# First conditioning product in two column halves, key projections between them, and conditioning steps of one load

## The chip, the cores and the metric

The kernel runs as one program on one core of a Trainium2 chip. The metric is the device time of an execution in microseconds (us). A timing is the median of several runs, and a profile is one further execution recorded by the hardware profiler.

The engines are TensorE (PE in the profile; PEld is its weight loading), VectorE (DVE), ScalarE (ACT), GpSimd (POOL) and SyncE (SP). SyncE issues every DMA of this kernel from one queue, in order.

## The reference

The reference is one inference step of a two-layer encoder trunk with width 1024. It handles a prompt of 1024 positions and eight sample sequences of 16 positions, 1152 token rows in all. Every sub-layer is modulated by a conditioning vector `c`: one vector for the prompt and one for each sample sequence, nine rows in all. This is the part that the change touches:

```python
sc = jax.nn.silu(c)
ada = (sc @ w_ada[l] + b_ada[l])[:, None, :]
sh_m, sc_m, g_m, sh_f, sc_f, g_f = jnp.split(ada, 6, axis=-1)
h = x * (1 + sc_m) + sh_m
qkv = h @ w_qkv_a[l]
...
x = layer_norm(DEEPNORM_ALPHA * x + (1 + g_m) * mix, ln_g[l, 0], ln_b[l, 0])
h = x * (1 + sc_f) + sh_f
f, conv_rows = conv_ffn(h, None if prompt else state_conv[l], w_up[l], conv_w[l], conv_b[l], w_down[l])
x = layer_norm(DEEPNORM_ALPHA * x + (1 + g_f) * f, ln_g[l, 1], ln_b[l, 1])
```

Layer 0 attends within a window, with 16 query heads and four key/value heads (256 key columns, 256 value columns), learned sinks, and a table of relative biases. Between the layers one key/value pair of width 1024 is projected, with a shift and a scale of its own. Layer 1 attends in a band. Each layer ends in a gated MLP of width 2816 with a causal convolution. In all there are seven conditioning products of 1024 x 2048: three per layer and one for the key/value pair.

## The kernel before

**Layout.** `H` holds the modulated input, transposed, as high and low halves: `split` (L166) copies a value to a rounded type (L157 or L159) and subtracts that copy from the value (L168). A product is then three matmuls for each slice of the contraction: weight-low by input-high, weight-high by input-low, weight-high by input-high. `mmT` (L267, matmul L272) takes 24 of them for a block of 384 tokens and 128 output columns; `mmX` (matmul L284) does the same with tokens on the output partitions. Weights come through `wload` (L170): a 512 KB load into one of two staging slots (`ws`), and a split into `wh` and `wl` on ScalarE and, by default, GpSimd.

**Order.** The program is written in one order, and a planner with a modelled timeline reorders the instructions of each engine's queue, the DMA queue included. On the chip every queue runs in the order it was given. `issue_after` ties an instruction behind another one, `high_priority` raises it, and `keep_in_program_order` fixes it among others so marked.

**A conditioning product, `ada` (L197).** The conditioning vectors, padded to 32 columns, are the stationary operand. For each of eight slices of the contraction, two loads of 512 KB bring 128 x 2048 weights, and four matmuls of 512 columns (L216) write four strips of 32 partitions of one PSUM bank, one strip of the array each. One step of the generator is one slice with its two loads. Then the bias comes, broadcast by four DMAs (L205), VectorE adds it (L228), TensorE transposes the row (L241), and VectorE copies nine columns for each 128 features into `adaT` (L243). Products 1, 2, 5 and 6 also send a gate row to DRAM.

**Opening, `build` (L1192).** Product 0 (shift and scale of layer 0) takes 16 weight loads, with the first key weight after six slices and the first of three blocks of x behind the last one; then follow its bias, the second key weight and the two other blocks. When `adaT` is complete, `affine` (L246) forms scale and shift (L253, L255). `first_h` (L1176) scales x: 24 tiles, eight 128-feature slices `c` in each of three blocks, on ScalarE (L1187), with the 128 sample rows of the third block on GpSimd (`sample_affine`, L917 and L918), and the splits into `H` on VectorE. Then come the key projections (`kproj`, six times 24 matmuls), the value projections (`vproj`, 216 matmuls of 256 columns), the first query projections (72 matmuls), and the scores (L514, L517). Keys and values go through DRAM (`kH`, `vH`) and back, and the biases through a skewed table in DRAM (`ska`) that `tables` (L1146) prepares. For the sample sequences, L648 makes their scores with four matmuls in four column strips, 144 columns wide in layer 0 and 272 in layer 1.

**Background.** Products 1 and 2 run as generators beside the attention of layer 0, one step each time an accumulated rate `BGA` passes one, with the two `ws` slots as their ring. Products 3 to 6 run beside the MLP of layer 0 at rate `BGF` per weight load, with a ring of three other buffers.

Of the kernel before, what the change touches and what calls it, by code (L numbers as in the profile page):

```python
# [10 lines left out]
F32 = mybir.dt.float32  # L11
# [22 lines left out]
BGA = 0.33  # L34
BGF = 0.72
# [59 lines left out]
class Trunk:  # L95
# [101 lines left out]
    def ada(self, gi, bank, ring=None, row=None):  # L197
# [3 lines left out]

        def load_bias(row):
            bsrc = self.I["adab"][gi : gi + 1, :]
            for j in range(4):
                nc.sync.dma_start(  # L205
                    row[32 * j : 32 * j + 32, 512:1024],
                    bass.AP(bsrc.tensor, bsrc.offset + j * 512, [[0, 32], [1, 512]]),
                )

        early = row is not None  # L210
        for k in range(8):
            w = [ring.next() for _ in range(2)]
            for hf in range(2):
                nc.sync.dma_start(w[hf], self.I["adaw"][gi, k, hf])
            for j in range(4):
                nc.tensor.matmul(  # L216
                    ps[32 * j : 32 * j + 32, :],
                    self.cT[:, k * 32 : k * 32 + 32],
                    w[j // 2][:, (j % 2) * 512 : (j % 2) * 512 + 512],
                    start=k == 0,  # L220
                    stop=k == 7,
                    tile_position=(0, 32 * j),
                )
            yield
        if not early:
            row = ring.next()
        load_bias(row)
        nc.vector.tensor_add(row[:, 0:512], ps, row[:, 512:1024])  # L228
        yield
        gate = {1: (0, 0), 2: (1, 2), 5: (2, 0), 6: (3, 2)}.get(gi)  # L230
        if gate is not None:
            g, j0 = gate
            for j2 in range(2):
                r = slice(32 * (j0 + j2), 32 * (j0 + j2) + 32)
                nc.gpsimd.tensor_scalar_add(row[r, 512:1024], row[r, 0:512], 1.0)
                nc.sync.dma_start(
                    self.gd[g, :, j2 * 512 : j2 * 512 + 512],
                    row[32 * (j0 + j2) : 32 * (j0 + j2) + 9, 512:1024],
                )
        for i in range(4):  # L240
            nc.tensor.transpose(ps[:, i * 128 : i * 128 + 128], row[:, i * 128 : i * 128 + 128], self.ident)  # L241
        dst = self.adaT[:, gi * 144 : gi * 144 + 144].rearrange("p (j i r) -> p i j r", j=4, i=4)
# [50 lines left out]
    def kproj(self, l, c, w, banks, tmp):  # L293
# [3 lines left out]
        for bi, (s0, n) in enumerate(BLK):  # L297
# [17 lines left out]
            if n > m:  # L315
                nc.sync.dma_start(self.kS[l][rows, :], t[:, m:n])
# [875 lines left out]
    def build(self):  # L1192
# [13 lines left out]
        for _ in range(6):  # L1206
            next(a0)
# [152 lines left out]
```

## Time and profile before

| | us |
|---|---|
| median of 3 runs | 2977.12 |
| lowest and highest run | 2976.96, 2980.3 |
| profiled execution | 2971.91 |
| its span | 2970.1 |
| PE, PEld busy in the span | 2849.4, 2529.7 |
| DVE, ACT, POOL busy | 1537.9, 1135.8, 911.0 |

The table sums one core's engines over the whole span. Busy matmul time overlaps itself in the pipeline, so PE at 96% of the span is not PE at its peak. The mean TensorE clock granted was 0.984 of full speed. DMA moved 353.90 MB. The opening, in which the DMA engines are loaded most, is the first 2.5% of the span.

In a row of the timeline the columns are start, length, engine, line, operation, output and input, shape, count, and in brackets the idle time before it and what ended it. A matmul of this kernel's plain 32-bit kind (L216, L648) leaves two records in the trace, so a step of four matmuls counts x8. In a row of groups the columns are line, engine, operation, names, shapes and count, then busy us and mean ns of one, then the idle time before them and what ended it.

### The profile page before, as it was taken

Reading aid. Unit: us, or ns where it says so; the run is one execution under the profiler, and the core shown is the slowest. Engines: PE = TensorE matmul, PEld = TensorE weight load, DVE = VectorE, ACT = ScalarE, POOL = GpSimd, SP = SyncE. Lnnn points to the kernel's source line nnn. Section 1 sums busy time; section 2 is a strip of 40 time slices with the busy share of each in tenths; the row PEclk is TensorE's granted clock in tenths of the full one; section 3 lists DMA queues with packets and bytes.
Section 4 is the critical chain, followed back from the end, with each engine's and each line's share of the span. In section 5 each row is a group of like instructions: output and inputs, shape, how many; then the busy total and the mean of one; then the engine's idle time right before and its main releaser. Section 6 shows DMA issues by size and latency. Waiting matters only on the chain.

```text
span 2970.1 us, 42557 instructions
## 1 busy us (share of the span) xinstructions
PE 2849.4 (96%) x16326; PEld 2529.7 (85%) x16326; DVE 1537.9 (52%) x3336; ACT 1135.8 (38%) x2352; POOL 911.0 (31%) x661
## 2 busy tenths in 40 slices
PE   6999899999999999999999999889999999999997
PEld 4987668899888898997999888767999999999986
DVE  4376768333443343459312667667724444444468
ACT  2465634332222222224435666652442222222224
POOL 3132423222222221254651111231422222222253
PEclk8999889999999999999999999999999999999998
DMA  8546353622222212223885456663311111111121
GB/s 302 182 146 188 100 167 127 227 76 77 97 71 99 92 69 75 82 71 110 285 289 181 121 151 192 185 209 126 133 43 43 43 40 42 43 43 38 41 83 77
DMA packets 175963, 353.90 MB, mean 119 GB/s; under 512 B 34680, under 2 KB 91832, under 8 KB 175504
## 3 DMA queue, kind: packets, MB, share of 16 engines
q1 hardware_dynamic: 175760, 351.19, 36.0%
q8 instruction: 128, 2.10, 0.3%
q14 instruction: 75, 0.61, 0.1%
HBM read 285.22 MB, written 75.35 MB: 121 GB/s over the span
## 4 chain that ended last, share of the span: by engine, by line
PE 80%; DVE 8%; DMA 3%; ACT 2%; issue 2%; POOL 2%; SPq 0%; DVEq 0%; ACTq 0%; POOLq 0%
PE PS L272 46%; PE PS L1065 16%; PE PS L284 7%; PE PS L564 3%; PE PS L542 2%; PE PS L216 2%; PE PS L514 1%; PE PS L517 1%; DVE F L481 1%; PE PS L683 1%; DMA F<-in_adaw_dram 1%; DVE acc L1125 1%; DVE F L954 0%; POOL acc L1124 0%; POOL wl L168 0%
## 5 line engine op out<-in xcount | busy, mean ns | idle before, releaser
L272 PE MATMUL PS<-H,wh 128*128 128x384 f32 (+1 forms) x5472 | 1045.4, 338 | 0.1
L272 PEld LDWEIGHTS PS<-H,wh 128*128 128x128 f32 x5472 | 966.7, 188 | 18.1 <-issue 7.9
L168 POOL TENSOR_TENSOR wl<-ws,wh 128x1024 fp32r<-128x1024 f32 x167 | 405.3, 2432 | 744.6 <-ACT wh L157 680.5
L994 DVE SCALAR_TENSOR_TENSOR F<-PS,F 128x256 f32<-128x256 f32 (+2 forms) x704 | 353.0, 512 | 533.2 <-ACT F L991 520.1
L272 PE MATMUL PS<-H,wl 128*128 128x384 f32 (+1 forms) x2736 | 565.0, 343 | 17.6 <-DVE H L159 8.2
L272 PEld LDWEIGHTS PS<-H,wl 128*128 128x128 f32 x2736 | 489.0, 190 | 49.9 <-issue 15.1
L991 ACT ACTIVATE F<-PS,F 128x384 f32<-128x384 f32 x264 | 177.5, 672 | 746.8 <-PE PS L272 745.2
L1065 PE MATMUL PS<-wh,X 128*128 128x512 f32 x1320 | 412.4, 394 | 9.6 <-DVE acc L1056 4.1
L1056 DVE TENSOR_TENSOR acc<-acc,PS 128x512 f32<-128x512 f32 x324 | 221.7, 686 | 271.6 <-PE PS L1065 271.1
L1040 POOL TENSOR_TENSOR F<-F 128x384 f32<-128x384 f32 x132 | 138.1, 1046 | 647.3 <-ACT F L1038 645.4
L1065 PEld LDWEIGHTS PS<-wh,X 128*128 128x128 f32 x1320 | 245.8, 188 | 63.1 <-issue 6.7
L157 ACT CAST wh<-ws 128x1024 fp32r<-128x1024 f32 x174 | 180.0, 1045 | 148.5 <-PE PS L1065 75.9
L1065 PE MATMUL PS<-wl,X 128*128 128x512 f32 x660 | 217.0, 393 | 0.0
L284 PE MATMUL PS<-wh,H 128*128 128x256 f32 (+1 forms) x936 | 170.4, 311 | 3.3 <-DVE H L168 2.3
L1065 PEld LDWEIGHTS PS<-wl,X 128*128 128x128 f32 x660 | 124.3, 188 | 28.1
L284 PEld LDWEIGHTS PS<-wh,H 128*128 128x128 f32 x936 | 135.0, 192 | 13.3 <-DVE H L168 3.0
L168 DVE TENSOR_TENSOR X<-F,X 128x384 fp32r<-128x384 f32 x110 | 97.1, 883 | 89.6 <-ACT X L157 89.3
L602 POOL TENSOR_TENSOR F<-F,x2att 64x512 f32<-64x512 f32 x62 | 79.3, 1279 | 191.4 <-DVE F L578 162.5
L542 PE MATMUL PS<-C,F 128*128 128x128 f32 x720 | 115.2, 286 | 20.7 <-DVE wh L549 11.4
L284 PE MATMUL PS<-x1att,H 128*128 128x512 f32 x504 | 132.4, 406 | 1.1 <-ACT x1att L157 0.5
L1038 ACT ACTIVATE F<-F 128x384 f32<-128x384 f32 x132 | 69.2, 524 | 143.7 <-DVE F L994 129.5
L542 PEld LDWEIGHTS PS<-C,F 128*128 128x128 f32 x720 | 85.4, 145 | 42.8 <-DVE wh L549 14.7
(213 smaller groups left out, 3448.0 us busy)
## 6 DMA issues: line engine op xcount, KB each, us to landing
ws<-in_wup_dram SPq DMA_DIRECT2D x88, 512.0 KB
F<-in_adaw_dram SPq DMA_DIRECT2D x74, 512.0 KB
ws<-in_wdn_dram SPq DMA_DIRECT2D x44, 512.0 KB
ws<-in_adaw_dram SPq DMA_DIRECT2D x32, 512.0 KB
x1att<-kH SPq DMA_DIRECT2D x60, 256.0 KB
xd<-F SPq DMA_DIRECT2D x27, 512.0 KB
F<-xd SPq DMA_DIRECT2D x27, 512.0 KB
vH<-X SPq DMA_DIRECT2D x40, 256.0 KB
```

The lines of the kernel that those rows point to most:

```text
L157: nc.scalar.copy(out, in_)
L168: self.eng(el).tensor_sub(lo, src, hi.bitcast(F32))
L272: self.nc.tensor.matmul(out[:, 0:n], w[a][:, k * 128 : k * 128 + 128], H[:, p, k, s0 : s0 + n], start=i == 0, stop=i == 23)
L284: self.nc.tensor.matmul(out[:, 0:n], H[:, p, j * kn + k, t0 : t0 + 128], w[a][:, k * n : k * n + n], start=i == 0, stop=i == 23,)
L542: nc.tensor.transpose(t[:, n * 128 : n * 128 + 128], p[:, (kt - k0) * 128 : (kt - k0) * 128 + 128], self.ident)
L564: mm = nc.tensor.matmul(ob[:, i0 * 128 : (i0 + n) * 128], vst[a][:, kt, :], pp[:, m * 128 : (m + n) * 128], start=cnt == 0, stop=cnt == to ...
L602: self.eng("v" if last else "p").tensor_mul(on[r, q], on[r, q], rb[r, :])
L991: nc.scalar.activation(y, ps[:, off : off + 384], AF.Identity, bias=w(3), scale=w(2))
L994: nc.vector.scalar_tensor_tensor(o, u, w(i), o, op0=ALU.mult, op1=ALU.add)
L1040: nc.gpsimd.tensor_mul(a, y, ya[bi])
L1056: nc.vector.tensor_add(row[:, n], row[:, n], ps)
L1065: nc.tensor.matmul(ps, ac[m][p][:, cs], w[m][q][:, n], start=i == 0, stop=i == 5)
```

## The change

- **Product 0** is made in two halves of its columns by a new function, `ada_half`. Half `h` holds shift and scale of the feature slices 4h to 4h + 3, and the weight columns are laid out on the host so that each half is eight loads of 512 KB. A half ends with its own add, two transposes, and the copies that form scale and shift, at high priority.
- **`opening`** replaces the start of `build`. It writes the loads in a fixed order: the weights of half 0, with the bias rows (two DMAs in place of four, from an array already broadcast on the host), the sinks and the first key weight among them; half a block of x; the second key weight; another half block; then the weights of half 1 with further half blocks of x between. x goes in 12 DMAs of 384 KB. All three blocks have buffers of their own.
- **Key projections** are split along the contraction: `mmT_part` with part 0 takes slices 0 to 3 as soon as half 0 is done, part 1 takes the rest, and six PSUM banks hold the partial sums. `kstore` is the second half of the old `kproj`. The second key weight's low part is made on VectorE in place of GpSimd.
- **`ada`** for products 1 to 6: one step is one load of 512 KB, with four matmuls of 256 columns that are tied behind the first of them and raised. The tail copies in two pieces. A gate row takes one GpSimd add in place of two, and four stores in place of two.
- **Rates**: `BGA` from 0.33 to 0.6 and `BGF` from 0.72 to 1.3, for about twice as many steps.
- The silu of the conditioning is computed for the nine used columns only, the rest being set to zero.

The diff, cut to its core:

```diff
-BGA = 0.33
-BGF = 0.72
+BGA = 0.6
+BGF = 1.3
...
-    def ada(self, gi, bank, ring=None, row=None):
+    def ada(self, gi, bank, ring=None):
+        lead = [None] * 4
         for k in range(8):
+                w = ring.next()
+                nc.sync.dma_start(w, self.I["adaw"][gi, k, hf])
+                for j in range(4):
+                    with ExitStack() as es:
+                        if lead[j] is not None:
+                            es.enter_context(self.tc.issue_after(lead[j]))
+                        if j:
+                            es.enter_context(self.tc.high_priority())
+                            es.enter_context(self.tc.issue_after(first))
+                        mm = nc.tensor.matmul(
+                            ps[32 * j : 32 * j + 32, hf * 256 : hf * 256 + 256],
+                            self.cT[:, k * 32 : k * 32 + 32],
+                            w[:, j * 256 : j * 256 + 256],
+                            start=k == 0 and hf == 0,
+                            stop=k == 7 and hf == 1,
+                            tile_position=(0, 32 * j),
+                            skip_group_check=True,
+                        )
+                    first = mm.ins if j == 0 else first
+                    lead[j] = lead[j] or mm.ins
+                yield
+        row = ring.next()
+        bsrc = self.I["adab"][gi : gi + 1, :]
+        for j in range(4):
+            nc.sync.dma_start(
+                row[32 * j : 32 * j + 32, 512:1024].rearrange("p (h x) -> p h x", h=2),
+                bass.AP(bsrc.tensor, bsrc.offset + j * 256, [[0, 32], [1024, 2], [1, 256]]),
+            )
         nc.vector.tensor_add(row[:, 0:512], ps, row[:, 512:1024])
         yield
+        gate = {1: (0, 0), 2: (1, 1), 5: (2, 0), 6: (3, 1)}.get(gi)
+            g, hf = gate
+            nc.gpsimd.tensor_scalar_add(row[:, 512:768], row[:, hf * 256 : hf * 256 + 256], 1.0)
+            for j in range(4):
+                nc.sync.dma_start(self.gd[g, :, j * 256 : j * 256 + 256], row[32 * j : 32 * j + 9, 512:768])
             nc.tensor.transpose(ps[:, i * 128 : i * 128 + 128], row[:, i * 128 : i * 128 + 128], self.ident)
+        dst = self.adaT[:, gi * 144 : gi * 144 + 144].rearrange("p (h j i r) -> p h i j r", h=2, j=4, i=2)
+        src = ps.rearrange("p (h i j r) -> p h i j r", h=2, i=2, j=4)
+        for h in range(2):
+            nc.vector.tensor_copy(dst[:, h], src[:, h, :, :, 0:9])
         yield
...
+    def mmT_part(self, w, out, s0, n, part):
+        for k in range(4 * part, 4 * part + 4):
+            for a, p in ((1, 0), (0, 1), (0, 0)):
+                self.nc.tensor.matmul(
+                    out[:, 0:n],
+                    w[a][:, k * 128 : k * 128 + 128],
+                    self.H[:, p, k, s0 : s0 + n],
+                    start=k == 0 and a == 1,
+                    stop=k == 7 and a == 0 and p == 0,
+                )
...
-            for c in range(2):
-                self.kproj(l, c, wk[c], kvb, kvt)
+            for bi, (s0, n) in enumerate(BLK):
+                for c in range(2):
+                    ps = self.bank(2 * bi + c)
+                    self.mmT_part(wk[c], ps, s0, n, 1)
+                    self.kstore(0, c, bi, ps, kvt)
...
-        ps = self.bank(1)
+        ps = self.bank(6)
...
-        s = I["sinks"]
-        nc.sync.dma_start(self.sink[:, 0:16], bass.AP(s.tensor, s.offset, [[0, 128], [1, 16]]))
-        nc.sync.dma_start(self.sink[:, 16:18], I["sinkS"])
-        nc.vector.tensor_scalar_mul(self.sink, self.sink, -1.0)
-        nc.sync.dma_start(self.sinkH, I["sinkH"])
...
+    def load(self, dst, src):
+        self.tc.keep_in_program_order(self.nc.sync.dma_start(dst, src))
+    def ada_half(self, h, bank, ring, row, t):
+        ps = self.bank(bank)
+        for k in range(8):
+            w = ring.next()
+            self.load(w, self.I["adaw"][0, k, h])
+            for j in range(4):
+                nc.tensor.matmul(
+                    ps[32 * j : 32 * j + 32, 0:256],
+                    self.cT[:, k * 32 : k * 32 + 32],
+                    w[:, j * 256 : j * 256 + 256],
+                    start=k == 0,
+                    stop=k == 7,
+                    tile_position=(0, 32 * j),
+            yield
+        with self.tc.high_priority():
+            nc.vector.tensor_add(row[:, 0:256], ps[:, 0:256], row[:, 256:512])
+            for i in range(2):
+                nc.tensor.transpose(ps[:, i * 128 : i * 128 + 128], row[:, i * 128 : i * 128 + 128], self.ident)
+            dst = self.adaT[:, 0:144].rearrange("p (w h c i r) -> p h i w c r", w=2, h=2, c=2, i=2)
+            src = ps[:, 0:256].rearrange("p (i w c r) -> p i w c r", i=2, w=2, c=2)
+            for i in range(2):
+                nc.vector.tensor_copy(dst[:, h, i], src[:, i, :, :, 0:9])
+            c = slice(36 * h, 36 * h + 36)
+            nc.vector.tensor_scalar_add(t[:, c], self.adaT[:, 72 + 36 * h : 72 + 36 * h + 36], 1.0)
+            nc.vector.tensor_copy(t[:, 72 + 36 * h : 72 + 36 * h + 36], self.adaT[:, c])
+    def first_h(self, t, x3, bi, h):
+        nc = self.nc
+        G, B = (t[:, o : o + 72].rearrange("p (c r) -> p c r", r=9) for o in (0, 72))
+        s0, n = BLK[bi]
+        m = min(n, 1024 - s0)
+        c0 = 4 * h
+        if n > m:
+            xm = x3[:, c0 : c0 + 4, m:n]
+            self.sample_affine(xm, xm, G, B, c0, 4, "p")
+        for c in range(c0, c0 + 4):
+            nc.scalar.activation(x3[:, c, 0:m], x3[:, c, 0:m], AF.Identity, bias=B[:, c, 0:1], scale=G[:, c, 0:1])
+            self.split(x3[:, c, :], self.H[:, 0, c, s0 : s0 + n], self.H[:, 1, c, s0 : s0 + n], "v", "v")
+    def opening(self):
+        nc, I = self.nc, self.I
+        ct = self.F[:, 12288:12544]
+        nc.sync.dma_start(ct, I["cT"])
+        row = [self.F[:, 10240 + 512 * h : 10752 + 512 * h] for h in range(2)]
+        ring = Ring([self.F[:, i * 1024 : i * 1024 + 1024] for i in range(10)])
+        x1 = self.x1p.tile([128, 9216], F32, name="x1in", tag="x1")
+        xs = [x1[:, i * 3072 : i * 3072 + 3072].rearrange("p (c t) -> p c t", t=384) for i in range(3)]
+        nc.gpsimd.memset(self.cT, 0.0)
+        s3, c3 = (t.rearrange("p (k r) -> p k r", r=32)[:, :, 0:9] for t in (ct, self.cT))
+        nc.scalar.activation(c3, s3, AF.Exp, scale=-1.0)
+        nc.vector.tensor_scalar_add(c3, c3, 1.0)
+        nc.vector.reciprocal(c3, c3)
+        nc.vector.tensor_mul(c3, c3, s3)
+        def xload(bi, h):
+            for c in range(4 * h, 4 * h + 4, 2):
+                self.load(xs[bi][:, c : c + 2, :], I["xT"][bi, :, c : c + 2, :])
+        def run(g, n):
+            for _ in range(n):
+                next(g, None)
+        t = self.gbr.next()
+        a = [self.ada_half(h, 6 + h, ring, row[h], t) for h in range(2)]
+        run(a[0], 4)
+        for h in range(2):
+            self.load(row[h][:, 256:512], I["adab0"][h])
+        s = I["sinks"]
+        self.load(self.sink[:, 0:16], bass.AP(s.tensor, s.offset, [[0, 128], [1, 16]]))
+        self.load(self.sink[:, 16:18], I["sinkS"])
+        self.load(self.sinkH, I["sinkH"])
+        nc.vector.tensor_scalar_mul(self.sink, self.sink, -1.0)
+        run(a[0], 2)
+        wk = [self.wload(I["wk0"][0], el="v")]
+        run(a[0], 2)
+        xload(0, 0)
+        wk.append(self.wload(I["wk0"][1], el="v"))
+        run(a[0], 1)
+        xload(1, 0)
+        for bi in range(3):
+            if bi < 2:
+                run(a[1], 4)
+            if bi == 0:
+                xload(2, 0)
+            if bi == 1:
+                xload(0, 1)
+            self.first_h(t, xs[bi], bi, 0)
+            s0, n = BLK[bi]
+            for c in range(2):
+                self.mmT_part(wk[c], self.bank(2 * bi + c), s0, n, 0)
+        run(a[1], 1)
+        xload(1, 1)
+        xload(2, 1)
+        nc.sync.dma_start(self.lnT, I["lnT"])
+        for bi in range(3):
+            self.first_h(t, xs[bi], bi, 1)
+        return wk
...
+        wk = self.opening()
...
+    aw = [w.reshape(8, 128, 2, 1024).transpose(0, 2, 1, 3) for w in aw]
+    aw[0] = aw[0].reshape(8, 2, 128, 2, 512).transpose(0, 3, 2, 1, 4).reshape(8, 2, 128, 1024)
+    z["adaw"] = np.stack(aw)
+    ab = g["b_ada"][0][:2048].reshape(2, 2, 2, 1, 256).transpose(1, 0, 2, 3, 4)
+    z["adab0"] = c(np.broadcast_to(ab, (2, 2, 2, 32, 256)).reshape(2, 128, 256))
```

More of the change, by code (lines that the diff above doesn't have):

```diff
@@ L200, in ada @@
         ps = self.bank(bank)
[L202 to L210, printed above, removed]
+        lead = [None] * 4
         for k in range(8):
-            w = [ring.next() for _ in range(2)]
             for hf in range(2):
[L214 to L224, printed above, removed]
@@ L225, in ada @@
-        if not early:
-            row = ring.next()
-        load_bias(row)
+                w = ring.next()
[18 more added lines that the diff above has]
+                    lead[j] = lead[j] or mm.ins
@@ L231, in ada @@
         if gate is not None:
[L232 to L239, printed above, removed]
+            g, hf = gate
+            nc.gpsimd.tensor_scalar_add(row[:, 512:768], row[:, hf * 256 : hf * 256 + 256], 1.0)
@@ L293, in kproj @@
     def kproj(self, l, c, w, banks, tmp):
-        nc = self.nc
-        o0 = (896, 512)[l]
-        rows = slice(c * 128, c * 128 + 128)
         for bi, (s0, n) in enumerate(BLK):
@@ new lines, in opening @@
+    def opening(self):
[43 more added lines that the diff above has]
+            self.first_h(t, xs[bi], bi, 0)
+            s0, n = BLK[bi]
+            for c in range(2):
[7 more added lines that the diff above has]
+        return wk
@@ L1194, in build @@
         self.bgrate = 0
-        ct = self.F[:, 12288:12544]
-        nc.sync.dma_start(ct, I["cT"])
-        nc.scalar.activation(self.cT, ct, AF.Exp, scale=-1.0)
-        nc.vector.tensor_scalar_add(self.cT, self.cT, 1.0)
-        nc.vector.reciprocal(self.cT, self.cT)
-        nc.vector.tensor_mul(self.cT, self.cT, ct)
-        x1 = self.x1p.tile([128, 9216], F32, name="x1in", tag="x1")
-        big = [self.F[:, i * 1024 : i * 1024 + 1024] for i in range(10)]
-        big = Ring(big + [x1[:, i * 1024 : i * 1024 + 1024] for i in range(3, 9)])
-        xs = [t.rearrange("p (c t) -> p c t", t=384) for t in (x1[:, 0:3072], self.F[:, 0:3072], self.F[:, 3072:6144])]
-        a0 = self.ada(0, 0, big, self.F[:, 10240:11264])
-        for _ in range(6):
-            next(a0)
-        wk = [self.wload(I["wk0"][0], el="v")]
-        for _ in range(2):
-            next(a0)
-        for c in range(0, 8, 2):
-            nc.sync.dma_start(xs[0][:, c : c + 2, :], I["xT"][0, :, c : c + 2, :])
-        for _ in a0:
-            pass
-        nc.sync.dma_start(self.lnT, I["lnT"])
-        wk.append(self.wload(I["wk0"][1]))
-        self.first_h(self.affine(0, (0, 1), e="v"), xs)
+        wk = self.opening()
         self.bg = [self.ada(1, 4), self.ada(2, 4)]
```

54 lines of the change are left out of this document (20 added, 34 removed).

## The prediction

> **What bounds the kernel now.** I read the page's shares and chain first, then a table of stretches, then the chain of waits and the timeline of the opening, then the groups by form.
>
> ```profile
> span 2970.1 us, 42557 instructions
> ...
> PE 80%; DVE 8%; DMA 3%; ACT 2%; issue 2%; POOL 2%; SPq 0%; DVEq 0%; ACTq 0%; POOLq 0%
> ```
>
> Four fifths of the chain that ends last are TensorE, so an edit counts if it frees TensorE time or lets its unbroken work start earlier. The stretches (columns: stretch, then length; busy us of PE, PEld, DVE, ACT, POOL; granted clock, DMA share, GB/s):
>
> ```profile
> 0.00:37.00 37.00, 17.76 (x68) 3.15 (x68) 7.42 (x9) 4.85 (x6) 3.03 (x7) 0.90 0.97 376
> 37.00:61.30 24.30, 19.99 (x81) 17.32 (x81) 21.14 (x45) 15.68 (x28) 20.94 (x18) 0.81 0.49 166
> 61.30:75.40 14.10, 14.00 (x66) 12.75 (x67) 4.62 (x10) 1.69 (x3) 4.28 (x3) 0.88 1.01 334
> 75.40:113.70 38.30, 38.30 (x289) 38.30 (x288) 6.51 (x14) 7.65 (x18) 2.99 (x5) 1.00 0.71 213
> 113.70:300.00 186.30, 183.88 (x1287) 148.32 (x1286) 124.30 (x411) 117.40 (x350) 44.83 (x49) 1.00 0.52 161
> ```
>
> For 37 us the DMA engines bind (0.97), then until 61.3 VectorE and GpSimd (21 of 24 us each), then TensorE without a gap. The chain of waits shows the join (start, length, what):
>
> ```profile
> 63.22 12.29 PE PS L272 x59
> 75.51 25.91 PE PS L284 x216
> 101.42 12.49 PE PS L272 x72
> ```
>
> Key projections, value projections, first query projections. At full rate 72 matmuls of 384 columns take 12.49 us, 0.173 each. The 144 of the key projections need 25 us, yet they run from 37 until 75.5. What starves them is in the rows of the opening: TensorE's weight steps, VectorE's end of the first product, ScalarE's first scaling of x, GpSimd's queue.
>
> ```profile
> 15.22 1.05 PE L216 MATMUL PS<-F,C 128*32 128x512 f32 x4 [0.24 <-DMA F<-in_adaw_dram]
> 16.50 1.05 PE L216 MATMUL PS<-F,C 128*32 128x512 f32 x4 [0.23 <-DMA F<-in_adaw_dram]
> ...
> 25.45 1.05 PE L216 MATMUL PS<-x1in,C 128*32 128x512 f32 x4 [0.23 <-DMA x1in<-in_adaw_dram]
> ```
>
> ```profile
> 31.20 0.69 DVE L228 TENSOR_TENSOR F<-PS,F 128x512 f32<-128x512 f32 x1 [8.59 <-DMA F<-in_adab_dram]
> 33.16 0.31 DVE L243 COPY C<-PS 128x144 f32<-128x144 f32 x1 [1.27 <-PE PS L241]
> 33.51 2.29 DVE L253 TENSOR_SCALAR C<-C 128x72 f32<-128x72 f32 x1
> 35.72 0.18 DVE L255 COPY C<-C 128x72 f32<-128x72 f32 x1
> ```
>
> ```profile
> 35.94 4.90 ACT L1187 ACTIVATE x1in<-x1in,C 128x384 f32<-128x384 f32 x8 [2.62 <-DVE C L255]
> ```
>
> ```profile
> 40.14 10.89 POOL L917 TENSOR_TENSOR F<-F,C 128x128 f32<-128x128 f32 x8 [4.39 <-DMA F<-in_xT_dram]
> 50.99 4.96 POOL L918 TENSOR_TENSOR F<-F,C 128x128 f32<-128x128 f32 x8
> 55.92 5.15 POOL L168 TENSOR_TENSOR wl<-ws,wh 128x1024 fp32r<-128x1024 f32 x2
> ```
>
> One 512 KB load is used every 1.28 us (410 GB/s). The product is complete at 26.5, its bias arrives only at 31.2, no column of x can be scaled before 35.9, and then all 24 tiles (three blocks of eight) crowd onto VectorE while GpSimd scales the sample rows of the last block until 56.
>
> **The opening, part by part.** The new order needs eight weight loads, not sixteen, for the first half of the columns. Ahead of the end of half 0 also stand one key weight (as now), the bias rows (256 KB as now, but early: 0.64 us at the pace) and three small sink loads (bounds 0 and one load's 1.28; I take the upper end, since their number, not their size, will count). So half 0 has its weights at 25.45 - 8 x 1.28 + 0.64 + 1.28 = 17.1. Its end now takes 35.94 - 31.20 = 4.74, of which L253 is 2.29 where its neighbour of the same size is 0.18; with no GpSimd split beside it I count 4.74 - 2.1 = 2.6, plus 0.6 for the last product step. ScalarE starts at 20.3 instead of 35.94.
>
> ```profile
> L216 PE MATMUL PS<-F,C 128*32 128x512 f32 x40 | 10.4, 727 | 7.2 <-DVE C L1200 5.8 <-DMA F<-in_adaw_dram 1.4
> ...
> L168 DVE TENSOR_TENSOR H<-x1in,H 128x384 fp32r<-128x384 f32 x8 | 4.3, 553 | 0.0
> ...
> L159 DVE CAST H<-x1in 128x384 fp32r<-128x384 f32 x8 | 2.7, 356 | 0.8 <-ACT x1in L1187 0.8
> ```
>
> A tile costs VectorE 0.553 + 0.356 = 0.91. The first half's 12 tiles take 10.9, and its 72 matmuls at the clock of 0.81 take 12.49 / 0.81 = 15.4: both fit between 20.3 and 37, under loads that run anyway. The second half's last weights land behind the second key weight and three half blocks of x (786 KB, 1.92 each): 25.45 + 1.28 + 5.8 + 1.9 = 34.4, and with 3.2 of product and end ScalarE starts it at 37.6. The bytes are the same, so the last of x lands at 40 as now. VectorE: 37.6 + 10.9 = 48.5, and some four evacuations of finished projections (one like L168 each) put it at 50.5. GpSimd now has half as many sample rows left: 40 + (10.89 + 4.96) / 2 = 48, then the two value weights, 5.15, until 53.2. TensorE can work off all but the last block's 24 matmuls (4.2 us) behind VectorE, of which I leave 3.5 to come after it: **54**. The value projections start at 54 instead of 75.5, a gain of 21.5.
>
> What is late next? By the table the DMA engines did 0.49 x 24.3 + 1.01 x 14.1 + 0.71 x 38.3 = 53.3 us of work between 37 and 113.7, where the scores begin. Now the scores would begin at 92.2, 52 us after the last of x. That cover is just gone. At the share of the first row (0.97) the work takes 55 us, 3 us too long; at 0.71 it takes 75 and eats the whole gain. Stores and bounces queue on SyncE's one queue behind each other's waits, but some of these bytes (caches, weights of the next products) are not for the first scores. I take 2.5, near the first row, because the stretch just before the value projections also runs at 1.01. Net: **-19**.
>
> The 4.72 MB of x now go in pieces of 384 KB. At the 512 KB pace they take 11.5 us. [...]
>
> **The steps of one load.** The other six products have 96 loads. The groups over the whole span, and three places of the timeline:
>
> ```profile
> L216 PE MATMUL PS<-F,C 128*32 128x512 f32 x296 | 53.2, 621 | 8.4 <-DVE C L1200 5.8 <-DMA F<-in_adaw_dram 2.6
> ...
> L216 PE MATMUL PS<-ws,C 128*32 128x512 f32 x128 | 30.9, 609 | 0.9 <-DMA ws<-in_adaw_dram 0.9
> ```
>
> ```profile
> 114.30 1.06 PE L216 MATMUL PS<-ws,C 128*32 128x512 f32 x8
> 115.29 1.66 PE L272 MATMUL PS<-H,wl 128*128 128x384 f32 x8
> ```
>
> ```profile
> 226.53 0.45 PE L648 MATMUL PS<-F 128*32 128x144 f32 x8
> 226.79 1.03 PE L216 MATMUL PS<-ws,C 128*32 128x512 f32 x4
> 227.75 0.33 PE L696 MATMUL PS<-C,F 128*128 128x128 f32 x1
> ```
>
> ```profile
> 1868.50 0.67 PE L648 MATMUL PS<-F 128*32 128x272 f32 x8
> 1869.10 0.50 PE L514 MATMUL PS<-x1att 128*128 128x512 f32 x1
> ```
>
> Each matmul is two records. A step's four matmuls write four column strips; together (x8) they hold TensorE 0.99 us, and two of them alone (x4) hold it 0.96. So a stretch costs about 0.98 whatever it holds, and the planner often parts a step. Subtracting the opening's ten F steps (10.4 us), 42.8 + 30.9 = 73.7 us at 1.06 each are 70 stretches, 68.4 us of TensorE, where 48 whole steps need 47. The change ties the four 256-column matmuls of a load to the first of them: 96 stretches. The same four-strip form takes 0.26 for 144 columns and 0.60 for 272, so 0.56 for 256, in bounds of 0.49 (half of 0.98) and 0.60. 96 x 0.56 = 53.8 against 68.4: 14.6 less (10.8 to 21.4). Not all of a busy TensorE is work: loads of weights cover 148.32 of 186.30 us in the attention, so I count four fifths, **-12** (-9 to -17).
>
> At nothing I count: two VectorE copies for one at the end of each product (as L243, 0.31, six more, under VectorE's 62 idle us of 186), one GpSimd add for two, and two more gate stores per product on SyncE. Uncovered they are about 2 us. The background's rates nearly double with the number of its steps, so it ends at the same place.
>
> **Sum.** -19 - 12 = -31. The profiled execution took 2971.9 (span 2970.1 and 1.8 around it); minus 31 is 2941. The median of the runs is 2977.1, 5.2 above the profiled one; I carry the same offset: **2946**.
>
> **Rivals.** *The four matmuls are parted again.* Then each part holds TensorE 0.56. Two parts per load are 192 x 0.56 = 107.5, 39 more than now, four fifths of it 31; less the opening's 19 that is +12, **2989**, slower. It decides from about 92 / 0.56 = 164 stretches for the 96 loads (68.4 + 19 / 0.8 = 92). For it: the planner parts 22 of 48 steps now. Against it: the new ties are written for exactly this order. 0.09.
>
> *The clock stays at half through the second half.* VectorE feeds TensorE in small bites there; 72 matmuls at half rate are 25 us, from 40 to 65, so 10.5 of the opening is left, with the transfers covered again: -10.5 - 12, **2955**. For it: 0.81 in the stretch where VectorE paces. Against: 0.81 is far from half. [...] 0.07.
>
> *The queue order is wrong.* If half 1's end is queued on VectorE ahead of first-half tiles, it blocks them until its weights land. In the worst case all 24 tiles come after 37.6: 37.6 + 21.8 + 2 + 3.5 = 65, the same **2955**. For it: the planner orders by modelled landings, and VectorE takes its queue in order. 0.08.
>
> *Transfers bind before the scores* (share 0.71): the opening gives nothing, -12, **2965**. 0.09.
>
> *The edits do not show*: the planner gives back elsewhere what it gains, **2977**. 0.05.
>
> **How the numbers follow.** The forecast has 0.62. Its own range is an opening of -12 to -23 and steps of -9 to -17, with 5 either way for the planner's changed order elsewhere: -45 to -16, 2932 to 2961. To take in three of the rivals and the lower bound of a stretch (-21 uncut), the range is 2928 to 2972; what lies above it is 0.14. A measurement of this kernel tells about 0.2% (6 us) from no change: faster is 0.62 + 0.07 + 0.08 + 0.09 = 0.86, same 0.05, slower 0.09.
>
> **What would show it.** Right: ScalarE's first scaling near 20, two bursts of VectorE tiles, the value projections starting at 50 to 58, scores at 90 to 98; the steps as stretches of eight records about 0.56 apart from their successor, about 96 of them. Wrong: value projections after 62; TensorE idle before the first scores, released by loads; stretches of two or four records; or a granted clock near 0.5 from 37 to 54.

## The result, and the profile after

The changed kernel takes 2953.65 us (median of five runs, 2949.16 to 2956.32), against 2977.37 for the kernel before, run beside it (2976.96 to 2980.3). The ratio is 0.9916, with a 95% interval of 0.9904 to 0.9927: 23.7 us faster. The forecast was 2946.0, its range 2928 to 2972. The profiled execution of the changed kernel took 2953.65 too. That of before took 2971.91, 5.2 below its median, so the two profiles differ by 18.3 us only.

The code has moved: the matmul of a step of products 1 to 6 is now L214, that of product 0 L1203, `mmT` L287, `mmT_part` L274, `mmX` L299, the scores L534 and L537, the scaling on ScalarE L1234, the end of a half L1213 to L1222, the key store L324, the skewed load L1187.

The page of after, span and shares of the chain:

```profile
span 2951.8 us, 43469 instructions
...
PE 79%; DMA 7%; DVE 5%; POOL 3%; ACT 2%; issue 2%; SPq 1%; DVEq 0%; POOLq 0%; ACTq 0%
```

The chain holds as much TensorE as before (79%, was 80%), but DMA's share has risen from 3 to 7%: the opening moved the other work ahead, and the transfers show. The stretches of after, cut where its own stages end:

```profile
0.00:20.80 20.80, 9.31 (x66) 1.93 (x66) 3.44 (x10) 2.60 (x3) 0.95 (x7) 1.00 0.89 334
20.80:42.90 22.10, 20.92 (x135) 14.47 (x136) 11.40 (x25) 7.92 (x13) 3.81 (x8) 1.00 1.03 401
42.90:60.00 17.10, 14.71 (x69) 12.77 (x70) 15.68 (x34) 10.36 (x18) 13.27 (x12) 0.90 0.29 80
60.00:70.00 10.00, 10.00 (x81) 10.00 (x80) 0.88 (x3) 2.44 (x5) 2.83 (x2) 1.00 1.02 335
70.00:106.10 36.10, 32.97 (x227) 32.77 (x226) 5.65 (x13) 7.55 (x18) 2.97 (x5) 0.95 0.85 267
```

From 20.8 to 42.9 TensorE and the DMA engines are both full (20.92 of 22.10 us; 1.03), while VectorE is busy 11.4. The clock of 1.00 in the first two rows must not be taken at its word: the first ten key projections take 3.9 us, from 21.98 to 25.86, 0.39 each, where later ones need 0.173. As slow are the first key projections of before: in the row below, which lists a clock of 0.50, four transposes take 1.09 us, and seven key projections, from 37.09 on, the other 2.73, 0.39 each.

```profile
30.00:40.00 10.00, 3.82 (x11) 2.93 (x12) 6.69 (x13) 5.10 (x8) 2.34 (x1) 0.50 0.99 388
```

From 42.9 to 60 the DMA engines are nearly idle (0.29), and just then they are full again (1.02). The timeline names both joints. First ScalarE's scalings in the two halves, then the last product step of half 1 on TensorE, then its add on VectorE:

```profile
20.82 2.50 ACT L1234 ACTIVATE x1in<-x1in,C 128x384 f32<-128x384 f32 x4 [4.63 <-DVE C L1222]
...
45.02 6.87 ACT L1234 ACTIVATE x1in<-x1in,C 128x384 f32<-128x384 f32 x12 [13.90 <-DVE C L1222]
```

```profile
42.22 0.64 PE L1203 MATMUL PS<-F,C 128*32 128x256 f32 x8
...
46.17 0.62 PE L274 MATMUL PS<-H,wl 128*128 128x384 f32 x2 [2.31 <-DVE H L159]
...
61.63 0.64 PE L299 MATMUL PS<-wh,H 128*128 128x256 f32 x4
...
76.42 0.74 PE L299 MATMUL PS<-wh,H 128*128 128x256 f32 x4 [3.13 <-DVE X L350]
```

```profile
42.95 0.42 DVE L1213 TENSOR_TENSOR F<-PS,F 128x256 f32<-128x256 f32 x1 [8.57 <-PE PS L1203]
```

The first half begins at 20.82. The second begins at 45.02, because VectorE stood for 8.57 us until TensorE came to the last step of half 1 at 42.22. That step has no bracket: TensorE was never idle before it, so it stood in TensorE's queue behind first-half key projections (its weights were issued at 25.52; in e5 below the last four steps run in one piece at 35.58). The value projections start at 61.63 (before: 75.51), the first scores at 106.1 (before: 113.7). Of the 13.9 us gained at the first of these points, 6.3 are lost on the way to the second. One gap takes 3.13. Short stretches of the same table show what comes with it (the eighth figure is the granted clock):

```profile
46.00:50.50 4.50, 4.27 (x14) 3.78 (x15) 4.46 (x10) 4.50 (x9) 3.37 (x6) 0.64 0.07 19
...
76.00:80.50 4.50, 4.08 (x25) 4.08 (x26) 1.22 (x3) 2.07 (x4) 1.77 (x1) 0.72 0.88 309
80.50:84.00 3.50, 3.50 (x27) 3.50 (x27) 0.42 (x1) 0.37 (x1) 0.61 (x1) 0.87 0.46 164
```

After the gap of 2.31 us that ends at 46.17, and again after that of 3.13, TensorE works at a reduced clock (0.64 over the next 4.5 us; 0.72 over 4.5 and 0.87 over 3.5). The second time costs, estimated from these clocks, 4.5 x 0.28 + 3.5 x 0.13 = 1.7 us. Of the 1.5 of the 6.3 that are left, 1.2 are no wait at all: in after 79 query projections stand ahead of the first score (92.40 to 106.10), in before 72 (12.49 us). The rest, 0.3, has no row of its own. The chain, and SyncE's queue at that place, say what the gap is:

```profile
60.65 14.79 DMA kH<-X
```

```profile
59.64 0.92 SPq L1187 DMA_DIRECT2D ska<-ea  x1
60.65 5.17 SPq L324 DMA_DIRECT2D kH<-X  x2
```

The skewed table of biases, read broadcast, is issued at 59.64, ahead of key stores. Until those have landed, the tile `X` cannot take the next evacuation: ScalarE's L349, which writes it, waits 9.99 us for `kH<-X`. So VectorE's reading of a finished PSUM bank is late (L350), for which the next value projection waits.

The steps of products 1 to 6 in after, by form, and three places of its chain:

```profile
L214 PE MATMUL PS<-F,C 128*32 128x256 f32 x512 | 37.1, 388 | 2.2 <-DMA F<-in_adaw_dram 2.2
L214 PE MATMUL PS<-ws,C 128*32 128x256 f32 x256 | 20.2, 399 | 4.2 <-DMA ws<-in_adaw_dram 4.1
```

```profile
118.57 0.57 PE PS L214 x8
119.14 0.20 PE PS L610
...
703.75 1.00 PE PS L214 x16
704.75 12.85 PE PS L287 x72
...
798.22 1.43 PE PS L214 x24
```

All but one of the 96 steps stay whole, eight records each (the one, at 212.15, is broken by sample scores, L668). A step by itself holds TensorE 0.57 us; two that meet hold it 1.00, three 1.43. Over the trace the 96 steps make 72 stretches and take 53.3 us where the forecast had 53.8, and the busy sums of the groups fall from 73.7 (42.8 + 30.9) to 57.3.

### The profile page after: what moved, and what is told of

It reads as the page before. It is cut to its first block, busy times and chain, and to the rows that moved or that the text cites. A ratio compares the mean times of both kernels' runs of the same rounds, so it can differ in the third digit from the quotient of the medians.

```text
span 2951.8 us, 43469 instructions
## 1 busy us (share of the span) xinstructions
PE 2826.3 (96%) x16774; PEld 2534.2 (86%) x16774; DVE 1530.0 (52%) x3349; ACT 1136.0 (38%) x2352; POOL 893.7 (30%) x657
## 4 chain that ended last, share of the span: by engine, by line
PE 79%; DMA 7%; DVE 5%; POOL 3%; ACT 2%; issue 2%; SPq 1%; DVEq 0%; POOLq 0%; ACTq 0%
PE PS L287 43%; PE PS L1085 16%; PE PS L299 9%; PE PS L584 2%; PE PS L562 2%; PE PS L214 2%; PE PS L534 1%; DMA F<-in_adaw_dram 1%; PE PS L537 1%; POOL wl L168 1%; DMA ws<-oN 1%; PE PS L703 1%; DMA F<-zd 1%; PE PS L902 1%; DVE acc L1145 1%
## 5 line engine op out<-in xcount | busy, mean ns | idle before, releaser
L287 PE MATMUL PS<-H,wh 128*128 128x388 f32 (+1 forms) x5376 | 1024.0, 338 | 0.0
L287 PEld LDWEIGHTS PS<-H,wh 128*128 128x128 f32 x5376 | 948.2, 188 | 10.4 <-issue 1.9
L287 PE MATMUL PS<-H,wl 128*128 128x384 f32 (+1 forms) x2688 | 550.0, 342 | 10.9 <-POOL wl L168 9.4
L287 PEld LDWEIGHTS PS<-H,wl 128*128 128x128 f32 x2688 | 477.0, 188 | 33.8 <-POOL wl L168 12.9
L299 PE MATMUL PS<-wh,H 128*128 128x256 f32 (+1 forms) x936 | 173.3, 314 | 7.6 <-DVE H L168 4.1
L299 PEld LDWEIGHTS PS<-wh,H 128*128 128x128 f32 x936 | 136.7, 194 | 18.0 <-DVE H L168 4.7
L299 PE MATMUL PS<-x1att,H 128*128 128x512 f32 x504 | 130.1, 399 | 4.2 <-ACT x1att L157 3.1
```

The lines of the kernel that those rows point to most:

```text
L287: self.nc.tensor.matmul(out[:, 0:n], w[a][:, k * 128 : k * 128 + 128], H[:, p, k, s0 : s0 + n], start=i == 0, stop=i == 23)
L299: self.nc.tensor.matmul(out[:, 0:n], H[:, p, j * kn + k, t0 : t0 + 128], w[a][:, k * n : k * n + n], start=i == 0, stop=i == 23,)
```

## The experiments

Each variant was timed beside runs of the kernel before: 2975.87 us for e1 to e4, 2976.57 for e5 to e8, 2978.08 for the last four. Ratios to before carry their 95% intervals; after has 0.9916.

**The two parts alone.** e1 has the new opening, with the old `ada` for products 1 to 6 and the old rates.

```diff
-BGA = 0.6
-BGF = 1.3
+BGA = 0.33
+BGF = 0.72
...
     def ada(self, gi, bank, ring=None, row=None):    # as in the kernel before
```

> The new opening with the old conditioning steps and rates. Theory 'two separate parts': the value projections start about 13.7 us earlier than before (61.6 for 75.4) and the first scores about 7.6 earlier, as in the changed kernel; 68 us of conditioning steps stay. So about 8 us less than before, 2969 (2964 to 2973). Rival 'it is all in the steps': no difference to before, 2977 (within 4 us).

Measured: 2971.83, ratio 0.9984 [0.9973, 0.9996], a gain of 4 us. Its value projections and first scores lie as early as in after (61.5 and 106.0). So part of those 7.6 us of lead is lost again later.

e2 has the old opening with the new steps: product 0 goes through the old `ada`, under the name `ada0`.

```diff
-        a0 = self.ada(0, 0, big, self.F[:, 10240:11264])
+        a0 = self.ada0(0, 0, big, self.F[:, 10240:11264])
```

> The old opening with the new steps of one load and the new rates for products 1 to 6. Theory 'two separate parts': the steps hold TensorE 53 us instead of 69, and nearly all of that reaches the end, 2962 (2959 to 2968). Rival 'it is all in the opening': within 4 us of before, 2977.

Measured: 2970.77, ratio 0.9977 [0.9967, 0.9987], a gain of 5 us, though its steps take 52.5 us of TensorE, as few as in after. The gain expected of the steps by themselves fell short, and 4 and 5 alone are far from the 24 together. In attention 0, between the first scores and a score matmul near its end, stretch by stretch (before, after, e2):

```profile
113.70:377.40 263.70, 249.86 (x1785) 199.51 (x1784) 183.67 (x601) 165.51 (x488) 77.89 (x77) 0.96 0.48 146
```

```profile
106.10:355.70 249.60, 235.45 (x1907) 197.99 (x1906) 176.83 (x603) 165.76 (x485) 74.15 (x76) 0.97 0.53 157
```

```profile
112.50:371.10 258.60, 239.47 (x1915) 199.63 (x1913) 180.66 (x603) 165.59 (x485) 72.77 (x75) 0.97 0.49 147
```

TensorE is relieved in both (249.9 to 235.5 and 239.5 us). In after its idle time stays (13.8, now 14.2), in e2 it rises to 19.1. The waits of e2 in that stretch say for what (us in total, times, longest):

```profile
PE PS L264 <- DMA ws<-in_adaw_dram: 8.8, 4, 3.0
```

Its steps wait 8.8 us for their weights, against 4.1 in after (the group above) and 0.9 before. That is 5 of the 9 us by which e2's attention 0 is longer than after's; the other 4 are busy time, and their cause stays open.

**The tie alone.** e3 is the kernel before, two loads and matmuls of 512 columns, with nothing but the tie (and the matmul on the last-loaded columns first); e4 is the kernel after without it.

```diff
-            for j in range(4):
-                nc.tensor.matmul(
+            for j in (3, 0, 1, 2):
+                with ExitStack() as es:
+                    if j < 3:
+                        es.enter_context(self.tc.high_priority())
+                        es.enter_context(self.tc.issue_after(first))
+                    mm = nc.tensor.matmul(
...
+                first = mm.ins if j == 3 else first
```

> The kernel before with only one edit: in a step of two loads the four matmuls of 512 columns are tied behind the one that uses the later load, so that a step is always one stretch. Theory 'the tie is what saves': 48 stretches of 0.99 make 47.5 us where 68.6 are now, 21 less on TensorE, of which four fifths reach the end: about 2960 (2955 to 2965). Rival 'the smaller load and the finer use of the two buffers save': nothing to see, 2977 (within 4 us).

Measured: 2956.35, ratio 0.9931 [0.9913, 0.9948], with 48 stretches of 1.0 us. An edit of a few lines in the old kernel gives 19.5 us, about as much as its steps give up on TensorE (68.6 us in 68 stretches before, 48.0 now).

```diff
-                        if j:
-                            es.enter_context(self.tc.high_priority())
-                            es.enter_context(self.tc.issue_after(first))
```

> The changed kernel without the ties of three matmuls behind the first in products 1 to 6. Theory 'the tie is what saves': the planner parts some of the 96 loads, to about 118 stretches of 0.555, 65 us where the changed kernel has 53: about 10 to 12 slower than the changed kernel, 2964 (2960 to 2968). Rival 'narrower matmuls save by themselves': as the changed kernel, 2953 (within 4 us).

Measured: 2964.09, ratio 0.9956 [0.9941, 0.9971]; the steps take 64.2 us, in 93 stretches where 118 were expected, and the MLP of layer 0 grows by 9.5 (836.9 against 827.4). Taking the tie away costs after 0.4% (0.9916 to 0.9956), and in the old kernel the tie by itself gains nearly what the whole change gains. The matmuls of 256 columns pay little without it: that MLP is longer than before's (828.8 and 831.9).

**The opening.** e5 ties the third block's first-half key projections behind the last product step of half 1, so that the half's end does not stand behind them.

```diff
+            self.lastmm = mm.ins        # in ada_half
...
+                if bi == 2:
+                    es.enter_context(self.tc.issue_after(self.lastmm))
                 for c in range(2):
                     self.mmT_part(wk[c], self.bank(2 * bi + c), s0, n, 0)
```

> The changed kernel; on TensorE the 24 first-half matmuls of the third block are tied behind the last step of half 1. In the changed kernel's trace half 1's last step stands at 42.2 behind them, though its weights were issued at 25.5. Theory 'queue order on TensorE': half 1 ends near 36, ScalarE starts the second half near 38 to 40 instead of 45.0, the first-half matmuls left over fill the wait, and the value projections start at 57 to 59 instead of 61.6; 2 to 4 less than the changed kernel, 2950. Rival 'TensorE is simply full there': ScalarE starts earlier, but the value projections still start at 61 to 62, no difference to the changed kernel.

Measured: 2948.71, ratio 0.9903 [0.989, 0.9917]; the second half starts at 42.44 instead of 45.02, the value projections at 59.81, a gap of 2.06 stays in them, the scores start at 103.2. ScalarE's start was expected at 38 to 40: the product ends earlier, but its transposes still wait (see e11). The total is 3.9 us better than after's by the ratios, whose intervals overlap, and the second profile of after has its first scores at 103.6; what e5 shows clearly are the two earlier starts.

e6 leaves the halves alone and makes the table and the skewed load early: the load is issued behind the last half block of x, so that it runs while the DMA engines were nearly idle. (The two later calls go, and the table takes another buffer and PSUM bank.)

```diff
         run(a[0], 2)
+        self.tables()
...
         xload(2, 1)
+        self.skew(0)
```

> The changed kernel; the bias table's product is made in the opening and the 3 MB skewed copy is issued right behind the last load of x instead of at 59.6. Theory 'the copy stands in front of the key stores': the 3.1 us gap of TensorE in the value projections (76.4 in the changed kernel) is gone, the copy fills the stretch from 43 to 60 in which the DMA engines are at 0.29, and the first scores come 3 to 6 earlier; 3 to 5 less than the changed kernel, 2949. Rival 'the stores are late by themselves': the gap stays, no difference to the changed kernel.

Measured: 2944.67, ratio 0.9887 [0.9871, 0.9903]. The load is issued at 38.96 instead of 59.64; the stretch from 42.9 to 60 has a DMA share of 0.79 instead of 0.29, and the chain has become what the forecast counted on:

```profile
46.99 14.09 PE PS L274 x70
61.08 25.91 PE PS L299 x216
86.99 13.70 PE PS L287 x79
```

```profile
42.90:60.00 17.10, 14.71 (x75) 13.45 (x72) 13.59 (x33) 10.37 (x18) 13.11 (x12) 0.90 0.79 249
```

The value projections run through in 25.91 us, as in the kernel before, and the scores start at 100.5, behind the same 79 query projections. e11 has both edits.

> The kernel after with both mended parts of the opening together: the second half's product steps tied ahead of the third block's first-half key projections, and the position table's matmul and the skewed load put ahead of the late transfers. Alone they gave about 5 and 9 us against after. Theory (two separate waits, one for DVE's second half at 45 and one of 3.1 us for key stores at 73): value projections start at 58 to 60, no wait of over 1 us of TensorE in them, first scores at 97 to 99; median 2940 to 2943. Rival (the late transfers bind: what the earlier end of the second half saves is waited for at the key stores): first scores at 100 to 101 and 2944 to 2946, no better than the early skew alone.

Measured: 2942.28, ratio 0.9871 [0.9843, 0.9899]; value projections at 58.5, no gap, first scores at 98.1. The two waits are separate and add: by the ratios e5 gains 3.9 us over after, e6 8.6 and both 13.4. Even so half 1 ends late, as VectorE's rows of e11 show:

```profile
38.74 0.42 DVE L1212 TENSOR_TENSOR F<-PS,F 128x256 f32<-128x256 f32 x1 [3.97 <-PE PS L1201]
42.94 0.30 DVE L1218 COPY C<-PS 128x36 f32<-128x36 f32 x2 [3.77 <-PE PS L1214]
```

The product is now added at 38.74, but its two transposes stand again behind key projections, 3.77 us.

**One load or two.** e7 is after's opening with e3's tied steps of two loads.

```diff
-                for j in range(4):
+            for j in (3, 0, 1, 2):       # 512 columns, two loads to a step
```

> The new opening, with steps of two loads and 512 columns as before, but tied so that each is one stretch. Theory 'stretches count': 48 stretches make about 48 us of TensorE, 5 less than the changed kernel's 53: 2949 (2945 to 2953). Rival 'single loads use the two buffers better': 2954 or more.

Measured: 2954.71, ratio 0.9925 [0.9912, 0.9938]: no better than after, so this expectation fell too. Against e3, whose steps are alike, the new opening gains only some 2 us (0.9931 to 0.9925, inside both intervals), though the first scores start at 104.7 instead of 113.2: 6.3 of these 8.5 us are lost by 567, in attention 0 and the stretch behind it. With the old steps the opening gained 4 (e1), with the new ones 18 (0.9977 in e2 to 0.9916). So an earlier first score is by itself no gain of that size at the end. e7 also showed where each kind of step is good. Its MLP is shorter and its attention 0 longer (257.0 against 249.6). The MLP's stretch, in e7 and in after:

```profile
566.60:1389.30 822.70, 815.35 (x4313) 731.20 (x4310) 374.17 (x649) 233.24 (x397) 255.05 (x186) 1.00 0.25 86
```

```profile
558.20:1385.60 827.40, 818.50 (x4529) 736.18 (x4526) 379.23 (x654) 233.04 (x398) 250.73 (x184) 1.00 0.26 86
```

This stretch repeats: 827.2 to 827.4 in all six profiles with the new opening and single tied loads (828.6 in e2), 822.7 in both kernels with two tied loads. e12 takes each where it is better, on top of e11: one load to a step for products 1 and 2, two for products 3 to 6.

```diff
-BGF = 1.3
+BGF = 0.72
...
-        self.bg = [self.ada(g, 7, fr) for g in (3, 4, 5, 6)]
+        self.bg = [self.ada2(g, 7, fr) for g in (3, 4, 5, 6)]    # e3's ada
```

> The kernel of both mended parts of the opening, and the conditioning steps of products 3 to 6 (in the MLP) taken back to two loads of 512 columns with the tie kept, at the old spacing, while products 1 and 2 (in attention 0) keep one load to a step. Theory (single loads help where TensorE waited for weights in attention 0, and in the MLP 32 tied stretches of 1.0 us cost less than 64 of 0.53 and 64 interruptions of the chain): a lead grown by 5 to 8 us between 583 and 1412, median 2934 to 2938. Rival (the MLP is bound by something else, and the gain of two loads in the MLP that an earlier variant showed was its run's chance): within 2 us of the kernel without this edit.

Measured: 2936.46 (four runs, 2936.08 to 2939.53), ratio 0.9856 [0.9832, 0.9879], 5.8 below e11 on the same chip. The MLP's stretch and a step in e12:

```profile
546.80:1371.10 824.30, 815.42 (x4313) 730.88 (x4310) 374.59 (x651) 233.56 (x398) 254.98 (x186) 1.00 0.26 87
```

```profile
705.95 1.00 PE PS L273 x8
706.95 4.31 PE PS L1138 x18
```

TensorE's busy time falls by 3.0 there against e11 (818.42 to 815.42), and so does the stretch. The lead over before grew by 4.5 between 583 and 1412 against the first profile of before, just under the 5 to 8 expected, and by 7.6 against the second. The rival's 2 us is out by the totals, but only 3.0 of the 5.8 lie in this stretch. The stretch ahead of it, in which product 3 begins, is 2.2 shorter in the profile (201.0 to 198.8); whether the edit did that stays open. It is the fastest kernel of this study.

**The end of attention 1.** Against the first profile of before, after lost 8 us of its lead between 1885 and the end. e8 put the third of layer 1's eight output-projection weight loads behind the last load of values.

```diff
+                if l == 1 and i == 2:
+                    es.enter_context(self.tc.issue_after(self.lastv))
                 w.append(self.wload(wo[i // 4, i % 4], el="ppppvvvv"[i], dst=d))
```

> The changed kernel; at the end of the second attention the third load of output weights is tied behind the last load of values, as the planner had it in the kernel before (in the changed kernel it stands in front and blocks SyncE's queue for 6.5 us). Theory 'a changed order of the queue loses 8 us there': the lead over the kernel before stays near 25 us behind this place instead of falling to 18; 4 to 8 less than the changed kernel, 2948. Rival 'the loss has another cause': no difference, 2953.

Measured: 2959.3, ratio 0.9937 [0.9924, 0.9951]. It gained nothing and rather lost; its stretch from 1885 to the end is 1093.4 us, after's 1093.2. The theory of crowded weight loads fell. Then both kernels were profiled again, unchanged.

> The kernel before, unchanged, profiled a second time. Open is what became of some 8 us between the end of attention 1's projections (about 1885) and the end, where the lead of the kernel after over before fell from 26.1 to 18.3 us, and where seven of the eight variants lost 4 to 8 us against the same one profile of before, whatever they change. Theory A (that first profile of before was lucky there; its own 2971.9 lies 5 us under its median): this second profile loses 3 to 7 us against the first from 1885 on and ends near 2976. Theory B (the changed kernels truly lose there): this profile keeps within 1 us of the first from 1885 to the end, wherever it stands before that.

> The kernel after, unchanged, profiled a second time, beside the second profile of before. By theory A (chance at the end of attention 1) the lead of after over before at 1885 and at the end differ by less than 4 us in this pair; by theory B the lead falls by 6 to 9 us again between the two marks.

The second profile of before took 2983.72, that of after 2950.85. The stretch from 1885 to the end in before's first and second profile and in after:

```profile
1884.80:2970.10 1085.30, 1041.65 (x5622) 944.58 (x5621) 573.44 (x1104) 370.86 (x675) 338.88 (x230) 0.99 0.23 77
```

```profile
1891.20:2981.90 1090.70, 1044.43 (x5622) 946.60 (x5620) 573.14 (x1104) 370.63 (x675) 338.53 (x230) 0.98 0.24 76
```

```profile
1858.60:2951.80 1093.20, 1042.30 (x5623) 946.16 (x5621) 573.86 (x1104) 370.96 (x676) 337.49 (x230) 0.98 0.24 76
```

The same program differs by 5.4 us in this stretch, which is two thirds of the 8 us that was to be explained; in the second pair the lead is 32.8 at 1885 and 32.9 at the end. So the first profile of before was probably lucky there. Two pairs of profiles speak for chance, with one correction: the second profile ended well above the 2976 expected of it, because it had lost 6.4 us more before 1885, between 377 and 1412. With two profiles each, the stages in us (marks are the starts of the same instructions in every trace):

| | before | after | difference |
|---|---|---|---|
| to the first scores | 113.7, 113.6 | 106.1, 103.6 | -8.8 |
| attention 0 to 377 | 263.7, 263.3 | 249.6, 250.2 | -13.6 |
| 377 to 583 | 205.8, 209.7 | 202.5, 204.8 | -4.1 |
| 583 to 1412 (MLP) | 828.8, 831.9 | 827.4, 827.3 | -3.0 |
| 1412 to 1885 | 472.8, 472.7 | 473.0, 472.5 | 0.0 |
| 1885 to the end | 1085.3, 1090.7 | 1093.2, 1090.6 | +3.9 |
| span | 2970.1, 2981.9 | 2951.8, 2949.0 | -25.6 |

The +3.9 is smaller than the spread within before; whether any of it is real stays open.

## Why the prediction came out near, and where its steps were wrong

The total came within 8 us (2953.65 for 2946), in the range. That was partly luck, for two errors leaned against each other: the opening gave less than half of its -19, and the stages with the steps gave more than their -12.

- **Half 0's end** was right: ScalarE's first scaling at 20.82, forecast 20.3.
- **"Both fit between 20.3 and 37"** failed, and it is the step from which the opening's error comes. The 72 first-half matmuls were costed alone (15.4 us). Half 1's eight product steps also stand in TensorE's queue there, seven at 0.57 and one at 0.99 on the chain, together 5.0, and the matmuls take 16.5, of which 2.1 come from the slow first ten. From their start at 21.98 that lasts until 43.4, not 37. So ScalarE's second half started not at 37.6 but at 45.02, and the value projections at 61.63 instead of 54. The forecast followed half 1 by its weights; what held it was its place in TensorE's queue. e5 moved that place and won 2.6 us of scaling start; e11 shows 3.8 more behind the transposes.
- **"I take 2.5"** for the transfers before the scores: of the 6.3 lost there, 4.8 are theirs, 3.1 for the gap and 1.7 for the clock behind it; 1.2 are the seven more query projections. The mechanism was named (stores and bounces behind each other on one queue), its size was set too near the lower end, and the clock behind a gap was not counted. The second profile of after shows the size of both: from the value projections to the scores TensorE stands idle for 2.37 us instead of 3.13, the clock of the whole stretch is 1.00 instead of 0.96, and it takes 42.2 us instead of 44.5. e6 shows the largest piece: the skewed load, ahead of the key stores in the queue. Moved into the stretch where the DMA engines are idle, it leaves value projections without a gap. So the opening's -19 was -7.6 in the first and -10.1 in the second profile of after.
- **0.56 for a step, 96 stretches**: the price was right (0.57) and so was the sum, 53.3 us for 53.8. The count was not: steps meet, so there are 72 stretches, and a step that follows another costs 0.43.
- **"I count four fifths, -12"** was too low: attention 0, the stretch to 583 and the MLP together gave -20.7 (of this the -4.1 is hardly larger than the spread of its stretch within before, 3.9). The forecast priced the steps as if the opening had no part in them. e1 and e2 say otherwise: each alone gave 4 to 5 us, both 24. The length of attention 0 is 265.2 in e1, 258.6 in e2 and 249.6 in after. Waits for step weights are half of the last difference; the rest is open, and no run here separates it from the order that the planner happens to find.
- **The offset of 5.2** was carried from before to after, and after had none. Before's profiled run was simply one of its fastest; its other runs reached 2989.66.

The rivals. *Four matmuls parted again*: no, all but one step of after are whole, and without the tie (e4) they took 64.2 us, not 107.5. *Clock at half*: the granted clock was 0.90 over 42.9 to 60, and 0.64 in its piece from 46 to 50.5, so the rival happened in little: 4.5 x 0.36 = 1.6 us of its 10.5. The clock fell there after 2.31 us without a matmul. In e6, with the same gap, the clock of that piece is 0.68. But the length of the gap alone does not decide it: in e7 TensorE waits 2.98 us in the value projections, and the clock of its stretch from 61.8 to 104.7 is 1.00. In e11 the gap at the place of after's 2.31 is 1.73, and the clock stays too:

```profile
44.90:47.00 2.10, 1.94 (x8) 1.29 (x8) 2.07 (x5) 2.10 (x4) 2.10 (x5) 1.00 1.14 338
47.00:50.00 3.00, 2.70 (x15) 2.71 (x16) 3.00 (x9) 3.00 (x7) 0.51 (x1) 1.00 1.09 361
```

*Queue order wrong*: half true, on another engine. It was TensorE's queue, not VectorE's, that blocked half 1, and it cost 7.6 of the 21.5, where the rival had 11. *Transfers bind*: in part, 4.8 for 2.5. *Edits do not show*: no.

For the loads of x in pieces of 384 KB the forecast kept the pace of before's 512 KB loads (410 GB/s). The stretch from 20.8 to 42.9, mixed of pieces of 384 and 512 KB, moved 401 GB/s at a share of 1.03, so the pace held.

## What to carry to other kernels

When a dependent product is cut in halves so that other work fits between, put the second half's last steps and its small tail (add, transposes) ahead of the filler in every queue that they cross, not only in the DMA queue: here the filler itself held back the half that it was waiting for. Transfers that nobody needs soon, but that must be early, belong into the stretch where the DMA engines are idle, and the trace's share column shows it (0.29 here). Before costing a new shape, try the cheapest piece of the change by itself: the tie of four matmuls in the old kernel gave 19.5 us where the whole change gave 23.7, and the parts of a change measured alone need not add up to it.

## What the runs showed of the hardware

In after a step of four 256-column matmuls in four column strips holds TensorE 0.57 us by itself, two in a row 1.00 and three 1.43: 0.43 a step and 0.14 for breaking into other work. A tied step of 512 columns holds it 1.00 in e12, so two single loads cost more than a double one only where they do not meet. Behind a short gap TensorE was slower in some of these profiles and not in others. In after the granted clock was 0.64 over 4.5 us behind a gap of 2.31, and 0.72 over 4.5 behind one of 3.13; in e6 it was 0.68 over 4.5 behind 2.31. In e5 16 value-projection matmuls took 3.52 us behind a gap of 2.06 (from 73.54, at a listed clock of 0.94 over 70 to 100), and the 16 after them 1.90. The clock stayed at 1.00 behind 1.73 us in e11 (44.9 to 50), and over the stretches with 2.37 idle us in the second profile of after and 2.98 in e7. Where it fell in after, the two waits of 2.31 and 3.13 us cost 1.6 and 1.7 more, estimated from these clocks. The granted clock that a profile lists should be held against the spacing of equal matmuls: after's reads 1.00 from 22 to 26, where the first ten key projections take 0.39 us each, and before's reads 0.50 from 30 to 40, where its first seven take as long. The same kernel spread by 18 us over its runs before (2971.88 to 2989.66) and by 7 after, while one stretch of 827 us repeated within 0.2 us in six profiles: a gain of 3 us can be read in such a stage where the spread of the whole hides it.
